# A transformer layer on one core: one product of the last matrix multiply, its order, and three sets of loads are rearranged

## The chip, the cores and the metric

The kernel runs on one core of one Trainium2 chip. The core has five engines with an instruction queue each: TensorE (PE) multiplies matrices, VectorE (DVE), ScalarE (ACT) and GpSimd (POOL) work on tiles, and SyncE (SP) issues the transfers between device memory and on-chip memory. Every queue is worked off in order, and an instruction that waits holds up all that stand behind it in its queue. Matrix products are summed in PSUM banks, here of 512 f32 columns.

The metric is device time in microseconds (us) of one execution. Beside the timed runs there is one execution under the hardware profiler, whose trace is read here.

## The reference

One layer of a model with 2048 tokens of width 1024, all in f32: a modulated norm, a projection to retention and attention heads, both mixers, an output projection, and then a feed-forward block that most of this document is about:

```python
x = x + g1 * (jnp.concatenate([ret, att], axis=-1) @ w_out)
h2 = _modulate(_rmsnorm(x, norm2_g), sh2, sc2)
x = x + g2 * (jnp.square(jax.nn.relu(h2 @ w_ff1)) @ w_ff2)   # 1024 -> 4096 -> 1024
return _rmsnorm(x, final_norm_g)
```

## The kernel before

**Arithmetic.** An f32 operand is split into an f16 part and an f16 remainder ("hi" and "lo"): ACT writes hi, and DVE or POOL writes lo. One product then takes three f16 matmuls: hi by hi, hi by lo, lo by hi. Both products of the feed-forward block are besides done with seven block products instead of eight (names P1 to P7): blocks are added and subtracted on POOL before, partial sums after. `ONTO` says which products are accumulated onto the PSUM bank of another: P6, P7 and P4 onto P1's, P3 onto P5's. In between, the running sum is read out ("tapped") for those output blocks that need it.

**Order.** The program is written out by hand. In the feed-forward block one step is one product: 12 matmuls of 512 columns, 4 blocks of the inner dimension by 3. A function call is put at a step and into a phase, and the phases of a step are emitted in the order

```python
FPHASES = ("begin", "pe", "sum", "hi", "lo", "relu", "out", "square", "late", "dma")
```

so `on(k + 1, "hi", f)` stands on its engine after all that belongs to step k. Nothing reorders it later. Tiles come from pools with a fixed number of buffers; a `Ring` strings several pools together and hands their buffers out in turn. A new tile waits until the last reader of its buffer is done.

**Up stage.** `w_ff1` is used in 16 blocks of 256 columns. `fetch_w1` loads a block in two tiles (names `w1r`), POOL adds (`sum_w1`, tiles `w1s`), ACT and DVE split (`w1f`). The token halves' seven forms (`hf`, 1 MB each) are loaded once. `up_out` taps a product on ACT (tile `r`), adds on DVE, squares on ACT, and `store_u` writes the result. `prelude` is the start of the stage: it loads the forms and does the first four products while the end of the attention part is still running. `w2_forms` runs beside blocks 8 to 15 and after: for each of the 16 row blocks of `w_ff2` it fetches two tiles (`b`), multiplies them by the gate on POOL, forms sums (`bs`), splits them (`w2f`) and stores them for the down stage (`wf`). The first tiles of the down stage's weights (`w`, `fetch_w2`) are loaded in the later part of the up stage.

**Down stage.** Four rounds of the inner dimension (`rd`), each with four passes `c`; a pass works on two pairs of token tiles (e = 0, 1), so there are 16 passes. `down` does P1, P6, P5, P7 and P3 for both pairs, 12 matmuls each. For P2 and P4 (`DEEP`) the two pairs are taken together and split once more, rows by pair, inner dimension and columns by halves: seven small products (`small`) of 6 matmuls with 256 columns, in four steps; POOL forms their sums in `sum_deep`. `down_out` and `small_out` add the PSUM sums to the output tiles `y`: directly on DVE (`plus`), or by ACT into a tile `d` that POOL adds (`tap`). In the last round `made` and `ending` finish each token tile: a sum of squares per half (ACT, `square`), the root on POOL, the final scaling of 1024 columns on DVE (`whole`), and the store (`out`). `P1`'s sums use a ring of 2 banks ("pc"), all others one of 6 ("pd").

Steps are counted from `NU`, the first of the down stage; pass c begins at step NU + 10 c. `STEPS` is the order of a pass's products; P2's small ones run with its first four steps and P4's from the sixth.

## Time and profile before

| | us |
|---|---|
| median of 3 runs | 2633.44 (2630.14 to 2634.4) |
| profiled execution, its own time | 2631.15 |
| span of its trace, first to last instruction | 2629.4 |
| TensorE busy in the span | 2574.5 (98%) |
| VectorE / GpSimd / ScalarE busy | 2170.5 / 1902.0 / 1608.5 |
| granted TensorE clock, mean | 0.997 |

By the trace the first matmul of the up stage starts at 1448.6, the first of the down stage at 2044.5, and the last round begins at 2466.6; the last matmul begins at 2617.5. In the lists of waits a line reads: engine, tile and line that waited, the engine, tile and line that released it, the total in us, the number of times, and the longest. In the timeline a row is start, duration, engine, line, instruction; a bracket gives the engine's idle time just before it and the releaser. In the table of windows a row gives the stretch and its length, then each engine's busy time and number of instructions, the granted clock, the busy share of the DMA engines and GB/s.

### The profile page before, as it was taken

Reading aid. Unit: us, or ns where it says so; the run is one execution under the profiler, and the core shown is the slowest. Engines: PE = TensorE matmul, PEld = TensorE weight load, DVE = VectorE, ACT = ScalarE, POOL = GpSimd, SP = SyncE. Lnnn points to the kernel's source line nnn. Section 1 sums busy time; section 2 is a strip of 40 time slices with the busy share of each in tenths; the row PEclk is TensorE's granted clock in tenths of the full one; section 3 lists DMA queues with packets and bytes.
Section 4 is the critical chain, followed back from the end, with each engine's and each line's share of the span. In section 5 each row is a group of like instructions: output and inputs, shape, how many; then the busy total and the mean of one; then the engine's idle time right before and its main releaser. Section 6 shows DMA issues by size and latency. Waiting matters only on the chain.

```text
span 2629.4 us, 47072 instructions
## 1 busy us (share of the span) xinstructions
PE 2574.5 (98%) x17193; PEld 1506.0 (57%) x17193; DVE 2170.5 (83%) x3160; ACT 1608.5 (61%) x2819; POOL 1902.0 (72%) x1611
## 2 busy tenths in 40 slices
PE   8999999998999999999999999999999999999997
PEld 5885555546666666666666444444444555555544
DVE  5778799769888888888885686899974789988898
ACT  3865454327778878887887676766766443333443
POOL 3644577627666678788787686899874688888886
PEclk9999999999999999999999999999999999999999
DMA  7877899756121223333333656777785768584741
GB/s 232 283 241 236 272 345 350 231 145 211 46 89 57 70 84 84 94 97 113 93 85 129 236 153 188 241 241 241 220 303 172 268 218 305 171 309 174 259 169 65
DMA packets 344816, 494.54 MB, mean 188 GB/s; under 512 B 90868, under 2 KB 215044, under 8 KB 340104
## 3 DMA queue, kind: packets, MB, share of 16 engines
q1 hardware_dynamic: 344568, 491.53, 56.7%
q8 instruction: 135, 2.21, 0.3%
q14 instruction: 97, 0.79, 0.1%
q10 hardware_dynamic: 16, 0.01, 0.0%
HBM read 328.18 MB, written 162.67 MB: 187 GB/s over the span
## 4 chain that ended last, share of the span: by engine, by line
PE 77%; DVE 8%; DMA 4%; POOL 4%; ACT 3%; issue 3%; SPq 0%; DVEq 0%; ACTq 0%; POOLq 0%
PE pso L1202 5%; PE pso L1203 5%; PE pso L1204 5%; PE pd L2407 5%; PE pd L2405 5%; PE pd L2406 5%; PE pu L2089 4%; PE pu L2091 4%; PE pu L2090 4%; PE st L219 4%; PE st L220 4%; PE o L254 4%; PE mp L186 4%; PE o L252 2%; DVE w2f L2209 2%
## 5 line engine op out<-in xcount | busy, mean ns | idle before, releaser
L199 DVE TENSOR_REDUCE nm<-mp 128x1 f32<-128x512 f32 x558 | 377.6, 684 | 97.6 <-PE mp L186 89.5
L225 ACT ACTIVATE p<-st 128x512 f32<-128x512 f32 x576 | 338.8, 594 | 140.1 <-PE st L220 139.3
L236 POOL TENSOR_TENSOR plo<-p,phi 128x1024 f16<-128x1024 f32 x160 | 348.2, 2182 | 70.5 <-ACT phi L229 69.3
L2089 PE MATMUL pu<-hf,w1f 128*128 128x512 f16 x896 | 340.2, 380 | 11.0 <-ACT r L2100 10.9
L2091 PE MATMUL pu<-hf,w1f 128*128 128x512 f16 x896 | 340.3, 380 | 0.0
L2090 PE MATMUL pu<-hf,w1f 128*128 128x512 f16 x896 | 340.2, 380 | 0.0
L229 ACT ACTIVATE phi<-p 128x1024 f16<-128x1024 f32 x288 | 302.8, 1051 | 0.0
L2405 PE MATMUL pd<-w,uf 128*128 128x512 f16 x640 | 242.6, 379 | 0.0
L2406 PE MATMUL pd<-w,uf 128*128 128x512 f16 x640 | 242.6, 379 | 0.0
L2407 PE MATMUL pd<-w,uf 128*128 128x512 f16 x640 | 242.6, 379 | 0.0
L238 DVE TENSOR_TENSOR plo<-p,phi 128x512 f16<-128x512 f32 x256 | 227.3, 889 | 15.2 <-ACT phi L229 13.4
L252 PE MATMUL o<-wv,plo 128*128 128x65 f16 x2304 | 230.0, 193 | 0.9 <-POOL plo L236 0.9
L254 PE MATMUL o<-wv,phi 128*128 128x129 f16 x2176 | 228.3, 220 | 0.0
L2439 ACT ACTIVATE d<-pd,scy 128x512 f32<-128x512 f32 x96 | 65.9, 687 | 261.6 <-PE pd L2407 256.2
L219 PE MATMUL st<-qr,ks 128*128 128x512 f16 x576 | 218.1, 379 | 3.7 <-ACT p L225 3.6
L252 PEld LDWEIGHTS <-plo 128*128 128x128 f16 x2304 | 205.1, 98 | 27.9 <-POOL plo L236 2.0
L2440 POOL TENSOR_TENSOR y<-y,d 128x512 f32<-128x512 f32 x96 | 148.5, 1547 | 98.1 <-ACT uf L2389 91.0
L220 PE MATMUL st<-qr,ks 128*128 128x512 f16 x576 | 218.2, 379 | 0.1
L1202 PE MATMUL pso<-wf,h_l 128*128 128x512 f16 (+1 forms) x576 | 208.2, 361 | 0.0
L1203 PE MATMUL pso<-wf,h_l 128*128 128x512 f16 (+1 forms) x576 | 208.1, 361 | 0.0
L1204 PE MATMUL pso<-wf,h_l 128*128 128x512 f16 (+1 forms) x576 | 208.1, 361 | 0.0
L254 PEld LDWEIGHTS <-phi 128*128 128x128 f16 x2176 | 193.1, 97 | 24.2
(414 smaller groups left out, 7025.7 us busy)
## 6 DMA issues: line engine op xcount, KB each, us to landing
wm<-in_w_ff SPq DMA_DIRECT2D x64, 512.0 KB, 6.7
u<-r SPq DMA_DIRECT2D x128, 256.0 KB, 4.5
wf<-w2f SPq DMA_DIRECT2D x128, 256.0 KB, 4.2
ur<-u SPq DMA_DIRECT2D x128, 256.0 KB, 5.8
y<-x SPq DMA_DIRECT2D x64, 512.0 KB, 6.9
w<-wf SPq DMA_DIRECT2D x28, 1024.0 KB, 6.7
w1r<-in_w_ff SPq DMA_DIRECT2D x48, 512.0 KB, 4.5
x<-y SPq DMA_DIRECT2D x48, 512.0 KB, 2.8
```

Source lines behind the costliest of these rows:

```text
L199: nc.vector.tensor_reduce(dst, src, axis=AX.X, op=ALU.max, negate=True)
L236: nc.gpsimd.tensor_tensor(lo, p, hi, op=ALU.subtract)
L252: mm(o[:, : HD + 1], lo[:, i, c], v[:, : HD + 1], start=False, stop=False)
L254: mm(o, hi[:, i, c], v[:, :VW], start=False, stop=last)
L1202: mm(ps[:, :width], hi[:, k], wh, start=k == 0, stop=False)
L1203: mm(ps[:, :width], hi[:, k], wl, start=False, stop=False)
L2089: mm(ps, whi, hi, start=k == 0 and at == i, stop=False, **go_on)
L2090: mm(ps, whi, lo, start=False, stop=False, **go_on)
L2091: mm(ps, wlo, hi, start=False, stop=k == 3, **go_on)
L2405: mm(ps, u[:, 0, b], w[:, b, 0], start=b == 0 and at == i, stop=False, **go_on)
L2406: mm(ps, u[:, 0, b], w[:, b, 1], start=False, stop=False, **go_on)
L2407: mm(ps, u[:, 1, b], w[:, b, 0], start=False, stop=b == 3, **go_on)
```

## The change

Five things are changed.

1. In the last round only P2 keeps the second level (`DEEP` becomes a list by round). P4 there is done for each pair directly, 12 matmuls of 512 columns, onto P1's bank. Its weights are written to memory without the second level's sums.
2. The order of the last round's products: P1 and P6 of both pairs, then P5, P7, P3, P4 of the first pair, then the same four of the second. A pass there has 12 steps instead of 10 (`START`). The final scaling of a second pair is written 3 steps later than it would follow, except in the very last.
3. In rounds 0 to 2, P7's sum is added to its two output blocks from PSUM by DVE (`plus` twice), not through ACT's tile `d` with an add each on POOL and DVE.
4. `w_ff1`'s second block is fetched 9 steps earlier and into buffers of the tag "hb".
5. `w2_forms` fetches its blocks 3 steps earlier, has four `bs` buffers instead of three, and does most of the second-level splits a step or two later; the down stage's first seven weight tiles are loaded every 6 steps instead of every 3.

Three small ones: `junk` comes from the ring of `d`, `bn` has two buffers, and the ring of the down stage's raw blocks has the new `bs` buffer too.

```diff
+    BLOCK = {P2: "a12", P4: "a22"}
+    DEEP = [(P2, P4)] * 3 + [(P2,)]
...
+        ff["bs"] = Ring((xp, "hu", 3), (ff["k"], "bs", 1))
...
-            w = xp.tile([P, D], F32, name="w1r", tag="xr", bufs=XR).rearrange("p (k n) -> p k n", k=4)
+            tag, bufs = ("hb", HB) if n == 1 else ("xr", XR)
+            w = xp.tile([P, D], F32, name="w1r", tag=tag, bufs=bufs).rearrange("p (k n) -> p k n", k=4)
...
-            on(b0 - 5 + g, "dma", fetch, g)
+            on(b0 - (8 if gate else 5) + g, "dma", fetch, g)
...
-                on(k + 1, "hi", hold)
-                split(k + 1, to[:, 0:4:3, s], lambda f: pieces(f, x[w][:, L], kept[i][:, L]))
+                on(k + 2, "hi", hold)
+                split(k + 2, to[:, 0:4:3, s], lambda f: pieces(f, x[w][:, L], kept[i][:, L]))
...
-            split(k + 1, to[:, 2:5:2, s], lambda f: pieces(f, kept[i]))
-            split(k + 2, to[:, 1:6:4, s], lambda f: pieces(f, x[w]))
-            on(k + 3, "sum", minus, held(L), part(L), held(L))
-            split(k + 4, to[:, 6, s], lambda f: pieces(f, kept[i][:, L]))
+            split(k + 2, to[:, 2:5:2, s], lambda f: pieces(f, kept[i]))
+            split(k + 3, to[:, 1:6:4, s], lambda f: pieces(f, x[w]))
+            on(k + 4, "sum", minus, held(L), part(L), held(L))
+            split(k + 6, to[:, 6, s], lambda f: pieces(f, kept[i][:, L]))
...
-        on(k0 + 10, "dma", fetch_w1, 1)
+        on(k0 + 1, "dma", fetch_w1, 1)
...
-            on(first[NB, 0] + 2 + 3 * i, "dma", fetch_w2, i)
+            on(first[NB, 0] + 2 + 6 * i, "dma", fetch_w2, i)
...
-    STEPS = [(i, e) for i in (P1, P6, P5, P7, P3) for e in range(2)]
+    STEPS = [[(i, e) for i in (P1, P6, P5, P7, P3) for e in range(2)]] * 3
+    STEPS += [STEPS[0][:4] + [(i, e) for e in range(2) for i in (P5, P7, P3, P4)]]
+    S3, S4 = [(0, 1)] * 3 + [(0, 4)], [(3, 4)] * 3 + [(1, 5)]
+    START = [10 * c if c < 13 else 12 * c - 24 for c in range(16)]
...
         elif i == P7:
-            d = tap(1, 1)
-            on(at + 1, "out", lambda: nc.vector.tensor_tensor(y[1, 0], y[1, 0], d, op=ALU.add))
+            if P4 in DEEP[PAIRS[p][0]]:
+                plus(1, 1)
+                plus(1, 0)
+            else:
+                tap(1, 1)
             made(at + 1, p, 1, 1)
+        elif i == P4:
+            plus(1, 0)
+            made(at, p, 1, 0)
...
-            junk = ff["sm"].tile([P, 512], BF16, name="junk", tag="junk", bufs=1)
+            junk = ff["d"].tile([P, 512], F32, "junk")
...
-            on(at + 1, "lo", whole, c)
-            on(at + 1 if n == 2 else at + 3, "dma" if n == 1 else "lo", store, c)
+            late = 3 if p % 2 and p < len(PAIRS) - 1 else 0
+            on(at + 1 + late, "lo", whole, c)
+            on(at + 1 if n == 2 else at + 3 + late, "dma" if n == 1 else "lo", store, c)
```

Three places show what this moves. A row is a line of the code, an instruction and its tiles; xN stands for N like it in a row.

SP's queue at the start of the up stage, before (`hf` are the seven forms, `w1r` the block of `w_ff1`, `x` a store of the attention part's result):

```order
L2076 DMA hf<-hf_230 128x4096
L2076 DMA hf<-hf_231 128x4096
L2076 DMA hf<-hf_232 128x4096
L2076 DMA hf<-hf_233 128x4096
L2076 DMA hf<-hf_234 128x4096
L1861 DMA x_212<-xr 128x1024
L2045 DMA w1r<-in_w_ff 128x4x256 x2
```

And now:

```order
L2079 DMA hf<-hf_230 128x4096
L2079 DMA hf<-hf_231 128x4096
L2048 DMA w1r<-in_w_ff 128x4x256 x2
L2079 DMA hf<-hf_232 128x4096
L2079 DMA hf<-hf_233 128x4096
L2079 DMA hf<-hf_234 128x4096
L1862 DMA x_212<-xr 128x1024
```

The two transfers of the second block stand ahead of the last three forms and of the store.

SP's queue in the later part of the up stage, before (`w` are the down stage's weights, `b` the tiles of `w2_forms`, `u` stores of the up stage's results):

```order
L2343 DMA w_24960<-wf_243 128x4096
L2132 DMA u_237<-r 128x4x128
L2213 DMA wf_270<-w2f 128x2x512
L2132 DMA u_238<-r 128x4x128
L2213 DMA wf_270<-w2f 128x512
L2343 DMA w_25021<-wf_244 128x4096
L2132 DMA u_240<-r 128x4x128
L2141 DMA b<-in_w_ff 128x1024
L2045 DMA w1r<-in_w_ff 128x4x256 x2
L2141 DMA b<-in_w_ff 128x1024
L2343 DMA w_25094<-wf_245 128x4096
```

And now:

```order
L2350 DMA w_24947<-wf_243 128x4096
L2135 DMA u_237<-r 128x4x128
L2144 DMA b<-in_w_ff 128x1024
L2135 DMA u_238<-r 128x4x128
L2144 DMA b<-in_w_ff 128x1024
L2135 DMA u_240<-r 128x4x128
L2048 DMA w1r<-in_w_ff 128x4x256 x2
L2350 DMA w_25076<-wf_244 128x4096
```

Both `b` tiles stand ahead of the second weight tile and of `w1r`, and the last stores of the second level (`wf_270`) are gone.

DVE's queue in the last round, where one pass ends and the next begins, before (L2500 is the final scaling, L2464 the read of a small product, L2435 the read of a large one, L2393 the lo part of a split, L2451 the add of `d`):

```order
L2435 SCALAR_TENSOR_TENSOR y<-pd,scy,y 128x512
L2393 TENSOR_TENSOR uf<-us,uf 128x512 x2
L2500 SCALAR_TENSOR_TENSOR y<-y,cy_e,g2b 128x1024 x2
L2464 SCALAR_TENSOR_TENSOR y<-pd,scy,y 128x256 x2
L2393 TENSOR_TENSOR uf<-us,uf 128x512
L2393 TENSOR_TENSOR uf<-ur,uf 128x256
L2500 SCALAR_TENSOR_TENSOR y<-y,cy_e,g2b 128x1024 x2
L2464 SCALAR_TENSOR_TENSOR y<-pd,scy,y 128x256 x2
```

And now (the same operations are L2512, L2476, L2442 and L2400):

```order
L2442 SCALAR_TENSOR_TENSOR y<-pd,scy,y 128x512
L2400 TENSOR_TENSOR uf<-us,uf 128x512 x2
L2476 SCALAR_TENSOR_TENSOR y<-pd,scy,y 128x256 x2
L2400 TENSOR_TENSOR uf<-us,uf 128x512
L2400 TENSOR_TENSOR uf<-ur,uf 128x256
L2476 SCALAR_TENSOR_TENSOR y<-pd,scy,y 128x256 x2
L2400 TENSOR_TENSOR uf<-us,uf 128x512
L2476 SCALAR_TENSOR_TENSOR y<-pd,scy,y 128x256 x2
L2400 TENSOR_TENSOR uf<-ur,uf 128x512
L2512 SCALAR_TENSOR_TENSOR y<-y,cy_e,g2b 128x1024
L2476 SCALAR_TENSOR_TENSOR y<-pd,scy,y 128x256
```

Two of the four final scalings that stood ahead of a pass's first two reads of small products now stand one by one behind the third pair of reads; the other two stand in the middle of the pass.

More of the change, by code (lines that the diff above doesn't have):

```diff
@@ L107, in layer_kernel @@
     ONTO = {P6: P1, P7: P1, P4: P1, P3: P5}
-    DEEP = {P2: "a12", P4: "a22"}
+    BLOCK = {P2: "a12", P4: "a22"}
+    DEEP = [(P2, P4)] * 3 + [(P2,)]
     wf_d = [
         [
-            dram.tile([P, 7, 2, 512] if i in DEEP else [P, 4, 2, 512], F16, name=f"wf{rd}{i}", tag=f"wf{rd}{i}")
+            dram.tile([P, 7, 2, 512] if i in DEEP[rd] else [P, 4, 2, 512], F16, name=f"wf{rd}{i}", tag=f"wf{rd}{i}")
             for i in range(7)
@@ L1684, in stats @@
             if 0 in hs:
-                x["st", c] = sm.tile([P, 4, 6], F32, name="bn", tag="bn")
+                x["st", c] = sm.tile([P, 4, 6], F32, name="bn", tag="bn", bufs=2)
                 x["mv", c] = sm.tile([P, 4, 2], F32, name="mv", tag="mv")
@@ L2149, in add @@
         def add(to, p, q, at=None):
-            x[to] = x[at] if at else xp.tile([P, 512], F32, name="bs", tag="hu", bufs=3)
+            x[to] = x[at] if at else ff["bs"].tile([P, 512], F32, "bs")
             nc.gpsimd.tensor_tensor(x[to], x[p], x[q], op=ALU.subtract)
         for g in range(2):
-            on(b0 - 5 + g, "dma", fetch, g)
+            on(b0 - (8 if gate else 5) + g, "dma", fetch, g)
             if gate:
@@ L2339, in fetch_w2 @@
             ff["w2"] = Ring((ff["h"][1], "hf", 7), (ff["h"][0], "hf", 7))
-        rd, (i, part) = n // 9, WS[n % 9]
+        rd, i, part, _ = WS[n]
         w = w2[rd, i, part] = ff["w2"].tile([P, 4, 2, 512], F16, "w2")
@@ L2345, in open_down @@
     def open_down():
[L2346 removed]
+        ff["raw"] = Ring((xp, "w1s", W1S), (xp, "hu", 3), (ff["k"], "bs", 1))
         ff["us"] = Ring((xp, "hp", HP), (xp, "u", 2), (ff["k"], f"k{P2}", 1), (ff["k"], f"k{P4}", 1))
@@ L2370, in sum_deep @@
     def sum_deep(c, i, which):
-        a1, a2 = (raw2[2 * c + e, DEEP[i]] for e in range(2))
+        a1, a2 = (raw2[2 * c + e, BLOCK[i]] for e in range(2))
         L, R = slice(0, 2), slice(2, 4)
@@ L2431, in down_out @@
         ps = pu[e, ONTO.get(i, i)]
-        y = {(g, n): ys[p, g][:, n * 512 : (n + 1) * 512] for g in range(2) for n in range(2)}
+        y = {(g, n): ys[p, g][:, n * 512 : (n + 1) * 512] for g in range(2) if (p, g) in ys for n in range(2)}
         def plus(g, n):
@@ L2507, in ending @@
             c = slice(i * D // n, (i + 1) * D // n)
-            on(at + 1, "lo", whole, c)
-            on(at + 1 if n == 2 else at + 3, "dma" if n == 1 else "lo", store, c)
+            late = 3 if p % 2 and p < len(PAIRS) - 1 else 0
+            on(at + 1 + late, "lo", whole, c)
+            on(at + 1 if n == 2 else at + 3 + late, "dma" if n == 1 else "lo", store, c)
     def down_jobs():
-        for n in range(36):
+        for n in range(7, len(WS)):
             if n < 9:
-                at = NU + n - 12
+                at = n - 12
             elif n < 14:
-                at = NU + 2 * n - 14
+                at = 2 * n - 14
             else:
-                at = NU + 10 * (4 * ((n - 14) // 9) + 3) + USED[(n - 14) % 9] + 1
-            if n > 6:
-                on(at, "dma", fetch_w2, n)
+                rd, _, _, used = WS[n - 14]
+                at = START[4 * rd + 3] + used + 1
+            on(NU + at, "dma", fetch_w2, n)
         on(NU - 12, "begin", open_down)
@@ L2525, in down_jobs @@
         for c in range(len(PAIRS) // 2):
-            s, p = NU + 10 * c, (2 * c, 2 * c + 1)
+            s, p = NU + START[c], (2 * c, 2 * c + 1)
+            rd = PAIRS[2 * c][0]
             for at, blk, e in ((-10, 0, 0), (-10, 0, 1), (-9, 1, 1), (-9, 1, 0), (-8, 2, 0), (-8, 3, 0), (-7, 2, 1), (-7, 3, 1)):
@@ L2533, in down_jobs @@
                 on(s - 2 + e, "sum", sum_u, p[e], "s2", "s1", "a11", ALU.subtract)
-                on(s + e, "sum", sum_u, p[e], "s3", "a11", "a21", ALU.subtract, "a21")
-                on(s + 3 + e, "sum", sum_u, p[e], "s4", "a12", "s2", ALU.subtract, "s2")
-            for k, i in ((-5, P2), (0, P4)):
+                on(s + S3[rd][e], "sum", sum_u, p[e], "s3", "a11", "a21", ALU.subtract, "a21")
+                on(s + S4[rd][e], "sum", sum_u, p[e], "s4", "a12", "s2", ALU.subtract, "s2")
+            for k, i in zip((-5, 0), DEEP[rd]):
                 for m in range(4):
                     on(s + k + m, "sum", sum_deep, c, i, m + 1)
-            for j, (i, e) in enumerate(STEPS):
+            for j, (i, e) in enumerate(STEPS[rd]):
                 split_u(s + j - 3, (c, i, e), lambda p=p[e], i=i: raw2[p, FORMS1[i]])
@@ L2542, in down_jobs @@
                 on(s + j, "out", down_out, s + j, c, i, e)
-            for k, i in ((0, P2), (5, P4)):
-                a1, a2 = (lambda p=q, i=i: raw2[p, DEEP[i]] for q in p)
+            for k, i in zip((0, 5), DEEP[rd]):
+                a1, a2 = (lambda p=q, i=i: raw2[p, BLOCK[i]] for q in p)
                 split_u(s + k - 3, (c, i, "ab"), a1)
```

9 lines of the change are left out of this document (4 added, 5 removed).

## The prediction

> **What bounds the kernel now.** I read the page first:
>
> ```profile
> span 2629.4 us, 47072 instructions
> PE 2574.5 (98%) x17193; PEld 1506.0 (57%) x17193; DVE 2170.5 (83%) x3160; ACT 1608.5 (61%) x2819; POOL 1902.0 (72%) x1611
> ```
>
> TensorE is busy 98% of the span. So only two things can matter: how much TensorE has to do, and the 55 us in which it does nothing. The list of TensorE's waits says where the larger part of those is:
>
> ```profile
> PE pd L2423 <- DVE y L2464: 10.9, 7, 1.8
> PE pu L2089 <- ACT r L2100: 10.9, 5, 3.9
> ```
>
> Five stalls in the up stage and seven in the down stage, 21.8 us. The rest is the start, which this change does not touch, and the end behind the last matmul. I looked at each of the three places in the timeline.
>
> **1. The second block of w_ff1.** The longest stall is at the start of the up stage (first fence), and it has a second cost:
>
> ```profile
> 1464.07 0.38 PE L2089 MATMUL pu<-hf,w1f 128*128 128x512 f16 x1 [3.94 <-ACT r L2100]
> 1464.55 0.63 PE L2091 MATMUL pu<-hf,w1f 128*128 128x512 f16 x1
> 1467.91 0.38 PE L2090 MATMUL pu<-hf,w1f 128*128 128x512 f16 x1
> 1464.00:1468.00 4.00, 3.93 (x11) 1.49 (x11) 1.43 (x2) 2.06 (x5) 4.00 (x4) 0.57 0.44 128
> ```
>
> After 3.94 us of idleness the granted clock is 0.57 in the next 4 us (last row, third number from the end). From 1464.55 to 1467.91 only eight matmuls start. At the usual pace of 0.216 us (below) they take 1.73, so 1.6 us more are lost. The cause is a load:
>
> ```profile
> 1435.51 9.13 SPq L2076 DMA_DIRECT2D hf<-hf  x7
> 1452.10 1.03 SPq L2045 DMA_DIRECT2D w1r<-in_w_ff  x2
> 1461.54 0.72 ACT L2062 ACTIVATE w1f<-w1r,sc 128x512 f16<-128x512 f32 x1 [6.76 <-DMA w1r<-in_w_ff]
> ```
>
> SP issues the block at 1452.10, behind seven forms and a store; ACT waits for it till 1461.54, and the tap that TensorE needs stands behind that wait on ACT. Now the block stands behind the fourth form, so it is issued some 11 us earlier, and ACT meets data that is there: **-3.94 and -1.6**. What it costs: the last three forms land later by 1 MB of w1r, one seventh of what the seven took, under 3 us. Their first user is the product that stalls now, so a form that came late would give back part of the 3.94; I take none. Bounds: 0 if the "hb" buffer is not free, -5.6 else. Both buffers were last read for forms that must be stored before the loads of the seven, so I take the full **-5.6**.
>
> **2. The later part of the up stage.** From 1880 to 1970 TensorE, ACT and POOL wait as follows, and the last row is the window in which the transfers are densest early on:
>
> ```profile
> PE pu L2089 <- ACT r L2100: 6.9, 4, 3.3
> ACT w2f L2205 <- POOL w2k L2228: 13.5, 6, 6.4
> POOL b L2147 <- DMA b<-in_w_ff: 18.7, 4, 10.5
> 1900.00:1920.00 20.00, 20.00 (x94) 9.06 (x93) 10.21 (x15) 12.88 (x22) 6.00 (x6) 1.00 1.01 336
> ```
>
> Read from the bottom: the DMA engines are full (1.01), because the early weight tiles of the down stage, 1 MB each, stand among the fetches of `b`. POOL waits 18.7 us for `b`, then ACT 13.5 us for POOL's second-level sums, and the tap behind it makes TensorE wait 6.9. The change acts on each link: `b` is fetched 3 steps (7.8 us) earlier and ahead of the second weight tile, the weight tiles come half as often, the ACT split is written a step later, and all four blocks of this stretch belong to round 3, whose P4 sums, splits and stores vanish. I take **-6.3**, nine tenths of the 6.9; bounds 0 and -6.9. Where the stall goes: what is late next is the weight tiles themselves, the last now issued 18 steps (47 us) ahead of the down stage, which covers a load of 7 us.
>
> An earlier fetch can also wait for its buffer. The tiles fetched at 1735.47 take the buffers that DVE last reads in the row of 1724.25:
>
> ```profile
> 1724.25 3.98 DVE L2209 TENSOR_TENSOR w2f<-b,w2f 128x512 f16<-128x512 f32 x2
> 1735.47 0.38 SPq L2141 DMA_DIRECT2D b<-in_w_ff  x1
> ```
>
> They are free at 1728.23, and 7.8 us before 1735.47 is 1727.7. SP waits some 0.5 us, with the stores of `u` queued behind it: no cost to TensorE, but no slack either (a rival below).
>
> **3. The last round.** Six of the seven waits of the down stage are here:
>
> ```profile
> PE pd L2423 <- DVE y L2464: 9.8, 6, 1.8
> 2506.99 2.48 DVE L2500 SCALAR_TENSOR_TENSOR y<-y,cy_e,g2b 128x1024 f32<-128x1024 f32 x2
> 2509.39 1.06 DVE L2464 SCALAR_TENSOR_TENSOR y<-pd,scy,y 128x256 f32<-128x256 f32 x2
> 2509.91 0.27 PE L2423 MATMUL pd<-w,uf 128*128 128x256 f16 x1 [1.59 <-DVE y L2464]
> ```
>
> Two final scalings stand on DVE ahead of the read of a small product, whose bank the next small product reuses. In the new order the first three pairs of reads have no scaling ahead of them: **-9.8**.
>
> TensorE's own work grows. The pace comes from three starts, 12 small matmuls and then 12 large ones:
>
> ```profile
> 2469.19 0.27 PE L2423 MATMUL pd<-w,uf 128*128 128x256 f16 x1
> 2470.50 0.38 PE L2405 MATMUL pd<-w,uf 128*128 128x512 f16 x1
> 2473.09 0.27 PE L2423 MATMUL pd<-w,uf 128*128 128x256 f16 x1
> ```
>
> 1.31/12 = 0.109 us and 2.59/12 = 0.216 us. P4 took 42 small matmuls, 4.58 us; now it takes 24 large ones, 5.18. In four passes **+2.4**. A pass is 12 x 2.59 + 4.58 = 35.7 us.
>
> Do the other engines keep up with 35.7? One period of the last round before (38.57 us, from stall to stall), ten passes of the earlier rounds, and DVE's groups in that period:
>
> ```profile
> 2511.22:2549.79 38.57, 35.39 (x206) 19.94 (x204) 37.29 (x44) 18.71 (x40) 35.03 (x31) 1.00 0.47 164
> 2100.00:2450.00 350.00, 350.00 (x2039) 199.29 (x2037) 316.43 (x380) 134.66 (x241) 291.54 (x221) 1.00 0.68 241
> L2393 DVE TENSOR_TENSOR uf<-us,uf 128x512 f16<-128x512 f32 x11 | 14.1, 1291 | 0.0
> L2464 DVE SCALAR_TENSOR_TENSOR y<-pd,scy,y 128x256 f32<-128x256 f32 x14 | 6.4, 474 | 1.1 <-PE pd L2425 0.9
> L2435 DVE SCALAR_TENSOR_TENSOR y<-pd,scy,y 128x512 f32<-128x512 f32 x4 | 3.0, 741 | 0.0
> L2451 DVE TENSOR_TENSOR y<-y,d 128x512 f32<-128x512 f32 x2 | 1.7, 834 | 0.2
> ```
>
> DVE, 37.3: off go P4's seven reads (3.3), two adds of `d` (1.7) and four splits, one of them half (some 4.5); on come two splits (2.6) and two reads (1.5): 31.9 of 35.7. POOL, 35.0: off go four 256-wide sums, 0.73 to 1.18 each (row below): 31 of 35.7. Both fit. Two banks now turn over faster: P3 follows its pair's P5 with one product between, 2.59 us, into which one read of 0.74 must fall behind a split and a scaling. I add **+0.8** for stalls there; bounds 0 and 9.8.
>
> In rounds 0 to 2 DVE gets four reads (3.0) for two adds (1.7), so 31.6 a pass becomes 32.9 of 35; POOL loses two adds a pass. TensorE does not wait in those ten passes at all (350.00 busy of 350.00), and I take 0; bounds 0 and +6.
>
> A rule speaks against the last round. POOL's and DVE's tile operations disturb each other; alone and together they take (shortest, median and longest in ns):
>
> ```profile
> L2393 DVE TENSOR_TENSOR uf<-us,uf x156: 673/1212/1765, 2052.9 to 2608.5; 128x512 f16<-128x512 f32 x156
> L2440 POOL TENSOR_TENSOR y<-y,d x96: 1258/1711/1743, 2052.4 to 2611.4; 128x512 f32<-128x512 f32 x96
> L2384 POOL TENSOR_TENSOR us<-ur x61: 716/726/1182, 2053.7 to 2594.2; 128x256 f32<-128x256 f32 x61
> L2500 DVE SCALAR_TENSOR_TENSOR y<-y,cy_e,g2b x18: 746/1274/1742, 2507.0 to 2622.9; 128x1024 f32<-128x1024 f32 x14, 128x512 f32<-128x512 f32 x4
> ```
>
> If such operations exclude each other for their whole length, a pass of the new last round needs, at their shortest, POOL's 14 full and 4 half ones (20.5) with some 3 for the four roots (one operation of a root takes 1.56 under a scaling, part 4), and DVE's 15.5 splits (10.4) and 4 scalings (5.1): 39 us, 3.3 above 35.7. In passes 13 and 14, which carry this whole load, that is +6.6 and a time of some 2617. The same count for the period before gives 14 full, 8 half, the roots, 17 splits, 2 adds and 4 scalings, 44 against 38.57 measured, so they overlap in part, and I do not take it. The Trainium skill states this exclusion (SBUF — State Buffer, section "SBUF: two separate sides": the pair of ports that VectorE and GpSimd share is a lock held for a whole instruction); by that sum these rows disagree.
>
> **4. The end.** Times from the last matmul's end at 2617.77:
>
> ```profile
> 2617.54 0.23 PE pd L2407
> 2618.53 5.12 DVE L2500 SCALAR_TENSOR_TENSOR y<-y,cy_e,g2b 128x1024 f32<-128x1024 f32 x6
> 2619.53 1.56 POOL L2494 TENSOR_SCALAR cv_e<-ss 128x1 f32<-128x1 f32 x1 [1.18 <-ACT junk L2483]
> 2621.69 3.32 SPq L2503 DMA_DIRECT2D out<-y  x6
> out<-y SPq DMA_DIRECT2D x4, 256.0 KB, 2.0
> ```
>
> Behind it come 11.6 us: six scalings, a root that POOL does in their shadow, six stores of 2 MB. Now the first pair is done four steps earlier. Left are the read (0.75), sum of squares (0.8), the root (some 1.1, under the first half tile's scaling), two half scalings of 0.75, and a store of 256 KB, 2.0 to landing. With 0.1 between links the last half is scaled at +4.5 instead of +5.9 (2618.53 + 5.12), issued 0.35 later and landed at +6.9. In the old end 2.4 us lie between the last issue with that landing time (2621.69 + 3.32 + 2.0) and the end of the span; part of it is the queue of 2 MB, and I take 1.5: 8.4. **-3.2**; bounds -2 and -4.4.
>
> **Sum**, against the profiled execution's own 2631.15 (its span is 2629.4): -5.6 - 6.3 - 9.8 + 2.4 + 0.8 - 3.2 = -21.7, so 2609.4. That execution lies inside the three runs (2630.14 to 2634.4, median 2633.44), so a median of new runs lies about there or a little above: **2610**.
>
> **Rivals.**
> - *The last round stays bound by DVE and POOL*: the sum of 39 holds in passes 13 and 14 and TensorE waits 3.3 in each, or the reads of P5 and P7 come late by about as much. For it: both engines over 90% busy before. Against: 3.8 us of room on DVE. Price +7 to +9: 2618. Chance 0.14.
> - *The up stage keeps its stalls*, because DVE, full from 1880 to 1900, is late whatever POOL does: 2610 + 6.3 = 2616. Chance 0.1.
> - *Rounds 0 to 2 start to stall*, DVE having one microsecond more a pass: half a microsecond in 12 passes, 2616. Chance 0.1.
> - *Slower than before*: the earlier fetch of `b` waits for its buffer in each of 14 blocks, the stores of `u` wait behind it on SP, the nine `r` tiles run out, and ACT's taps stop TensorE. It decides once SP waits longer than about 8 us, three steps, in which four of the nine `r` tiles are due; 2 us in each block is 28: 2638. The row of 1724.25 allows 0.5 us of waiting, so 0.03.
>
> Forecast 0.58; the rest, 0.05, are mixtures. From the forecast's bounds (2604 with all stalls gone and -4.4 at the end, 2613) to the rivals at 2616 and 2618 the range is 2603 to 2620. A measurement tells 0.2% (5.3 us) from no change. Only the last rival and a mixture reach it: faster 0.93, same 0.04, slower 0.03.
>
> **What would show it.** The wait of 3.94 and the clock of 0.57 are gone at the start of the up stage, and w1r is issued near 1440. POOL's waits for `b` are short past 1900, and TensorE is busy throughout. In the last round no L2464-like wait remains and passes are 35.7 apart; DVE is at 90% or less. The span ends 8 to 9 us behind the last matmul. I am wrong if a new wait of the large products on DVE appears in the last round, if rounds 0 to 2 take more than 35.0 a pass, or if SP waits in front of `b`.

## The result

| | before | after |
|---|---|---|
| median of the runs (us) | 2632.73 (2630.14 to 2634.4) | 2619.19 (2617.96 to 2620.43) |
| ratio, 95% interval | | 0.9949 (0.9932 to 0.9967) |
| profiled execution, its own time | 2631.15 | 2618.28 |
| span of its trace | 2629.4 | 2616.4 |

The change makes the kernel 13.5 us faster. That lies inside the range of the prediction, at its upper end, 9 us above the forecast of 2610. So more than a third of the expected gain is missing, and the first question is where.

The page of the changed kernel, and its list of TensorE's waits (engine, tile and line that waited, who released it; total us, times, longest):

```profile
span 2616.4 us, 46757 instructions
PE 2577.8 (99%) x17121; PEld 1499.6 (57%) x17121; DVE 2133.8 (82%) x3142; ACT 1594.3 (61%) x2779; POOL 1842.2 (70%) x1563
```

```profile
PE pu L2092 <- DVE r L2107: 9.4, 2, 7.1
...
PE pu L2092 <- ACT r L2103: 1.6, 2, 1.1
...
PE pd L2412 <- DVE y L2442: 0.6, 3, 0.2
```

The waits of the down stage have gone from 10.9 us to 0.6. Those of the up stage were 10.9 and are 11.0: one of them now lasts 7.1 us. The two profiled executions, stretch by stretch, by the start of the first matmul of each:

| stretch | before | after | difference | predicted |
|---|---|---|---|---|
| until the up stage (code hardly touched) | 1448.6 | 1446.5 | -2.1 | 0 |
| up stage, first 126 matmuls | 35.0 | 38.5 | +3.5 | -5.6 |
| rest of the up stage | 560.8 | 559.1 | -1.7 | -6.3 |
| rounds 0 to 2 | 422.1 | 420.8 | -1.3 | 0 |
| last round to its last matmul | 150.8 | 143.6 | -7.2 | -6.6 |
| behind the last matmul | 11.6 | 7.5 | -4.1 | -3.2 |
| sum | | | -12.9 | -21.7 |

The down stage and the end did what was forecast, the up stage did not. The first row is code in which only `bn`'s second buffer and the early transfer are new; the up stage starts at 1446.5 to 1451.7 in the twelve experiments below, so the difference is scatter between executions, and stretches are compared from their own start.

The two rows of the up stage scatter as well. Of the experiments below, e4 and e12 have this stage as in the kernel before, e3, e5 and e6 as in the changed one. The first 126 matmuls take 35.0, 36.0 and 36.1 in the three traces of the old stage and 38.5, 39.0, 37.9 and 38.0 in the four of the new; the rest takes 560.8, 564.8 and 562.1 against 559.1, 559.1, 559.0 and 557.4. By these means the differences are +2.6 and -3.9 rather than +3.5 and -1.7.

**The start of the up stage, after.** The timeline of the changed kernel: SP's queue, the links of the chain, and TensorE:

```profile
1438.18 1.19 SPq L2048 DMA_DIRECT2D w1r<-in_w_ff  x2
1439.42 6.67 SPq L2079 DMA_DIRECT2D hf<-hf  x3
1449.57 0.32 SPq L1862 DMA_DIRECT2D x<-xr  x1
1460.68 1.12 POOL L1872 TENSOR_SCALAR xr<-xr,cy_f 128x1024 f32<-128x1024 f32 x1 [9.22 <-DMA x<-xr]
1462.76 1.26 POOL L2060 TENSOR_TENSOR w1s<-w1r 128x512 f32<-128x512 f32 x1
1466.27 1.95 ACT L2065 ACTIVATE w1f<-w1s,sc 128x512 f16<-128x512 f32 x3 [7.61 <-POOL w1s L2060]
1469.60 0.68 DVE L2107 TENSOR_TENSOR r<-pu,r 128x512 f32<-128x512 f32 x1
1470.33 0.58 PE L2092 MATMUL pu<-hf,w1f 128*128 128x512 f16 x1 [7.12 <-DVE r L2107]
```

and a row of its table of windows:

```profile
1468.00:1472.00 4.00, 1.67 (x5) 0.55 (x5) 4.00 (x6) 2.62 (x5) 1.13 (x1) 0.50 1.02 328
```

The second block of `w_ff1` is issued at 1438.18 as planned, and ACT no longer waits for it. But POOL scales `xr` in place, and may do so only when the store of `x` out of that tile has landed. That store is issued at 1449.57 and lands 11 us later, behind the forms and the block. Then POOL makes the sums `w1s` of the second block, ACT and DVE split them, DVE adds a product that stands behind the split in its queue, and only then TensorE has a bank again. It idles 7.12 us, and its clock is granted at 0.50 afterwards (third number from the end of the last row).

Was that chain there before? Yes, and it was on time by a hair:

```profile
1460.27 1.12 POOL L1871 TENSOR_SCALAR xr<-xr,cy_f 128x1024 f32<-128x1024 f32 x1 [6.70 <-DMA x<-xr]
1470.39 0.68 DVE L2104 TENSOR_TENSOR r<-pu,r 128x512 f32<-128x512 f32 x1
1470.71 0.38 PE L2091 MATMUL pu<-hf,w1f 128*128 128x512 f16 x1
1471.13 0.38 PE L2089 MATMUL pu<-hf,w1f 128*128 128x512 f16 x1
```

These are the same instructions in the kernel before. DVE is through at 1471.07, TensorE starts at 1471.13, 0.42 behind the matmul before it instead of 0.216: it had already waited 0.2 us for this chain. That matmul, the 73rd of the stage, starts 22.49 us behind the first one before and 23.79 after. The wait of 3.94 us that was removed had only covered this one. Of the 3.5 us that the 126 matmuls lose, 1.3 are lost up to this matmul; the other 2.2 are lost behind it, where the clock is granted at 0.50: the remaining matmuls take 14.7 us instead of 12.5.

### The profile page after: what moved, and what is told of

The parts are those of the page before. It is cut to its first block, busy times and chain, and to the rows that moved or that the text cites. A ratio compares the mean times of both kernels' runs of the same rounds, so it can differ in the third digit from the quotient of the medians.

```text
span 2616.4 us, 46757 instructions
## 1 busy us (share of the span) xinstructions
PE 2577.8 (99%) x17121; PEld 1499.6 (57%) x17121; DVE 2133.8 (82%) x3142; ACT 1594.3 (61%) x2779; POOL 1842.2 (70%) x1563
## 5 line engine op out<-in xcount | busy, mean ns | idle before, releaser
L2412 PE MATMUL pd<-w,uf 128*128 128x512 f16 x672 | 254.7, 379 | 0.6 <-DVE y L2442 0.6
L2414 PE MATMUL pd<-w,uf 128*128 128x512 f16 x672 | 254.7, 379 | 0.0
L2413 PE MATMUL pd<-w,uf 128*128 128x512 f16 x672 | 254.7, 379 | 0.0
L2447 POOL TENSOR_TENSOR y<-y,d 128x512 f32<-128x512 f32 x72 | 107.3, 1493 | 136.0 <-ACT uf L2396 126.1
L187 PE MATMUL mp<-ks,qr 128*128 128x512 f16 x512 | 194.0, 379 | 1.4 <-DVE nm L200 0.6
```

What stands on the lines that cost most here:

```text
L2412: mm(ps, u[:, 0, b], w[:, b, 0], start=b == 0 and at == i, stop=False, **go_on)
L2413: mm(ps, u[:, 0, b], w[:, b, 1], start=False, stop=False, **go_on)
L2414: mm(ps, u[:, 1, b], w[:, b, 0], start=False, stop=b == 3, **go_on)
```

## The experiments

Each is the kernel named with the edit shown; e9 and e10 join two, and e11 undoes several. The ratio is to runs of the kernel before on the same chip, whose median there lay between 2632.4 and 2635.2; "up" is the time from the first matmul of the up stage to the first of the down stage, "down" from there to the start of the last matmul, "end" what follows that matmul's end.

| run | median (us) | ratio (95%) | up | down | end |
|---|---|---|---|---|---|
| before | 2632.73 | | 595.8 | 572.9 | 11.6 |
| after | 2619.19 | 0.9949 (0.9932 to 0.9967) | 597.6 | 564.4 | 7.5 |
| e1, three forms later | 2612.27 | 0.9922 (0.9906 to 0.9939) | 589.3 | 564.4 | 7.5 |
| e2, w_ff1's block late again | 2615.98 | 0.9935 (0.9921 to 0.9950) | 592.2 | 564.4 | 7.5 |
| e3, scaling not delayed | 2620.03 (one run) | | 598.0 | 565.4 | 7.5 |
| e4, before + delayed scaling | 2646.04 | 1.0049 (1.0034 to 1.0064) | 600.7 | 585.6 | 11.6 |
| e5, pairs interleaved | 2619.82 | 0.9946 (0.9931 to 0.9961) | 596.9 | 564.8 | 8.8 |
| e6, P7 through ACT's tile | 2619.39 | 0.9944 (0.9929 to 0.9958) | 595.4 | 566.0 | 7.5 |
| e7, b late again | 2617.18 | 0.9935 (0.9921 to 0.9950) | 592.6 | 564.4 | 7.5 |
| e8, weight tiles dense again | 2619.08 | 0.9944 (0.9927 to 0.9961) | 596.0 | 564.4 | 7.5 |
| e9, both of these | 2616.75 | 0.9940 (0.9925 to 0.9955) | 593.1 | 564.4 | 7.5 |
| e10, e1 and e7 together | 2609.23 | 0.9913 (0.9898 to 0.9928) | 585.3 | 564.4 | 7.5 |
| e11, last round as before | 2622.32 | 0.9964 (0.9949 to 0.9978) | 594.6 | 566.4 | 11.6 |
| e12, before + P7 from PSUM | 2626.09 | 0.9966 (0.9953 to 0.9978) | 598.2 | 566.3 | 11.6 |

### The start of the up stage: e1 and e2

e1 fetches the last three forms behind the store of `x`, with the block of `w_ff1` still early:

```diff
-            on(k0 + i // 2, "dma", fetch_h, i)
+            on(k0 + i // 2 if i < 4 else made_at + 1, "dma", fetch_h, i)
```

> The changed kernel, with the last three forms (P7, P3, P4 of hf) loaded behind the store of x instead of ahead of it. Theory (the new stall of 7.1 us at the start of the up stage hangs on that store: it stands behind 8 MB in the queue, POOL waits 9.2 us for it before it may form w1's sums, and the sums are what ACT, DVE and then TensorE wait for): the store lands some 3 us after its issue, POOL starts 6 to 8 us earlier, the stall and the slow clock behind it go, -8 to -9 us, some 2610.5. Rival 1 (the store takes 11 us whatever is ahead of it, or POOL's sums wait for something else): the stall stays, 0. Rival 2 (the forms now come too late for the fifth product): a stall on the forms' transfer of 1 to 4 us takes its place, -4 to -8.

Measured: 2612.27, 7 us less than the changed kernel. The same chain in its timeline:

```profile
1450.90 0.34 SPq L1862 DMA_DIRECT2D x<-xr  x1
1451.28 1.78 SPq L2079 DMA_DIRECT2D hf<-hf  x3
1454.68 1.32 POOL L1872 TENSOR_SCALAR xr<-xr,cy_f 128x1024 f32<-128x1024 f32 x1 [1.89 <-ACT w1f L2065]
1465.46 0.38 PE L2092 MATMUL pu<-hf,w1f 128*128 128x512 f16 x1 [0.93 <-DVE r L2107]
```

The store, issued ahead of the three forms, lands within 4 us; POOL's `xr` starts 3.8 us behind the issue instead of 11.1, and TensorE waits 0.93 instead of 7.12, with no loss of clock. So the queue in front of the store of `x` made the new wait, and no wait for the later forms takes its place. The first 126 matmuls take 30.1 us, 4.9 less than before.

e2 undoes the fetch of the second block alone:

```diff
-            tag, bufs = ("hb", HB) if n == 1 else ("xr", XR)
-            w = xp.tile([P, D], F32, name="w1r", tag=tag, bufs=bufs).rearrange("p (k n) -> p k n", k=4)
+            w = xp.tile([P, D], F32, name="w1r", tag="xr", bufs=XR).rearrange("p (k n) -> p k n", k=4)
...
-        on(k0 + 1, "dma", fetch_w1, 1)
+        on(k0 + 10, "dma", fetch_w1, 1)
```

> The changed kernel with part 4 undone (w_ff1's second block fetched where it was, into the old buffers). Theory (the early fetch removed one wait and uncovered a longer one on POOL's sums, by delaying the store of x): the wait of 3.9 us with its slow clock comes back in place of the 7.1 with its slow clock, -3 us, some 2616. Rival, as predicted before the result (the early fetch is worth 5.6 us, and the long wait has another cause, the other edits or this run): +5.6 us on top of the 7.1, or no change at all.

Measured: 2615.98. The old wait is back, and yet the kernel is 3.2 us faster than with the early fetch:

```profile
1466.62 0.38 PE L2092 MATMUL pu<-hf,w1f 128*128 128x512 f16 x1 [3.71 <-ACT r L2103]
```

Part 4 of the change, as it stands, is a loss. Together with the forms moved as in e1, the early fetch is 3.7 us better than e2, which has neither. The forms moved alone, with the block still late, were not run, so how the 3.7 us divide between the two is not shown.

### The last round: e3, e4, e5, e11 and e12

The last round gave what was predicted. The question was which part of the change gave it. I had said: the scalings no longer stand ahead of the reads of the small products. e3 takes the delay of the scalings away from the changed kernel. e4 gives the kernel before a delay alone, there for both pairs of token tiles and not only for the second:

```diff
-            late = 3 if p % 2 and p < len(PAIRS) - 1 else 0
+            late = 0
```

> The changed kernel with the final scaling of a second pair written where it would follow (the shift by 3 steps undone), the new order and the direct P4 kept. Theory (place: what stands on DVE ahead of the first reads of small products decides): one scaling of 1.2 to 1.4 us instead of two stands ahead of each of two reads; two cost 1.6 to 1.8 us, so the slack was 0.7 and one costs 0.4 to 0.6, twice in three passes: waits of small products of some 3 us in total. Rival (load: the stalls came from DVE having more than it could do in a pass, and P4's removal cured them): no such waits, 0.

```diff
-        v, r = (sm.tile([P, 1], F32, name=f"c{x}_e", tag=f"c{x}_e") for x in "vy")
+        v, r = (sm.tile([P, 1], F32, name=f"c{x}_e", tag=f"c{x}_e", bufs=6) for x in "vy")
...
-            on(at + 1, "lo", whole, c)
-            on(at + 1 if n == 2 else at + 3, "dma" if n == 1 else "lo", store, c)
+            late = 3 if p < len(PAIRS) - 2 else 0
+            on(at + 1 + late, "lo", whole, c)
+            on(at + 1 if n == 2 else at + 3 + late, "dma" if n == 1 else "lo", store, c)
```

> The kernel before, with one edit: in the last round all final scalings but those of the last pass are written 3 steps later (and the tiny root tiles have more buffers, which that needs). P4's second level and the order stay. Theory (place): the six waits of 9.8 us go without the 2.4 us of added TensorE work, -8 to -10 us against before. Rival (load): DVE is busy 37.3 us of a period of 38.6 and cannot do that in the 35.1 that a pass takes TensorE, so at least 2 us in each of three passes come back elsewhere: -3 us at most.

Measured, e3: three waits of 0.54 us return and the down stage takes 1.0 us more, which lies between the theory's 3 us and the rival's 0. e4: the kernel becomes 13 us slower than before, where both theories had it faster. DVE and TensorE in one place of e4's last round (for e4 the line numbers are those of before):

```profile
2521.26 3.96 DVE L2500 SCALAR_TENSOR_TENSOR y<-y,cy_e,g2b 128x1024 f32<-128x1024 f32 x2
2525.15 0.47 DVE L2464 SCALAR_TENSOR_TENSOR y<-pd,scy,y 128x256 f32<-128x256 f32 x1
2525.54 1.36 DVE L2393 TENSOR_TENSOR uf<-ur,uf 128x512 f16<-128x512 f32 x1
2526.83 1.76 DVE L2393 TENSOR_TENSOR uf<-us,uf 128x512 f16<-128x512 f32 x1
2528.51 3.95 DVE L2500 SCALAR_TENSOR_TENSOR y<-y,cy_e,g2b 128x1024 f32<-128x1024 f32 x2
2536.37 0.37 PE L2423 MATMUL pd<-w,uf 128*128 128x256 f16 x1 [6.19 <-DVE y L2464]
```

and the next period in its table of windows:

```profile
2536.37:2580.40 44.03, 37.55 (x205) 20.81 (x205) 37.73 (x42) 18.56 (x40) 36.46 (x31) 0.93 0.41 143
```

A pair of scalings takes 3.95 us where it took 2.48 before: the delayed ones stand beside an unbroken row of POOL's operations. In the 44.03 us of the period DVE is busy 37.73 and idle the rest, waiting for TensorE in turn (38.57 and 37.29 before). The clock adds to it: it is granted at 0.93 in this row (third number from the end), and of the 12.7 us that the down stage takes more than before, longer waits are 6.7. A delay that makes room at one read takes it from the next reads. So a delay of the scalings is not what cured the last round, as far as these two runs show; other places for them were not tried.

e5 keeps P4 direct, but takes the pairs in the old, interleaved order:

```diff
-    STEPS += [STEPS[0][:4] + [(i, e) for e in range(2) for i in (P5, P7, P3, P4)]]
+    STEPS += [STEPS[0] + [(P4, e) for e in range(2)]]
```

> The changed kernel, with P4 at one level in the last round, but with the two pairs' products interleaved as before (P5, P5, P7, P7, P3, P3, P4, P4 of the two pairs). It tells whether the end (7.5 us behind the last matmul instead of 11.6) comes from ending the pairs one by one, as I argued, or from P4's form. My theory: with P4 of the two pairs as the last two products, the first pair's second tile is finished 2.6 us before the second pair's, so DVE has one scaling of 1.3 to 2.5 us more in the end: the end grows by 2 to 4 us, 2621 to 2623 (2619.2 with the order). The rival: the two reads of P4's bank are the end in any order, and the end stays within 1 us: 2619 to 2620. Either order has the same matmuls, so the passes stay at 36.0.

Measured: 0.4 us more in the down stage, 1.3 more behind the last matmul, the median unchanged (2619.82). The order carries the smaller part of the gain at the end; the rival is nearer.

e11 puts the whole last round back as it was and keeps all else. Its core:

```diff
-    DEEP = [(P2, P4)] * 3 + [(P2,)]
+    DEEP = [(P2, P4)] * 4
...
-    STEPS += [STEPS[0][:4] + [(i, e) for e in range(2) for i in (P5, P7, P3, P4)]]
-    S3, S4 = [(0, 1)] * 3 + [(0, 4)], [(3, 4)] * 3 + [(1, 5)]
-    START = [10 * c if c < 13 else 12 * c - 24 for c in range(16)]
+    S3, S4 = [(0, 1)] * 4, [(3, 4)] * 4
+    START = [10 * c for c in range(16)]
...
-            late = 3 if p % 2 and p < len(PAIRS) - 1 else 0
+            late = 0
```

> The changed kernel with the last round as before (P4 at a second level, the pairs interleaved, no delay of the scalings, places 10 apart) and all else as changed: P4's second-level sums, splits and stores for round 3 are back in the up stage too. My theory: the down stage's six waits return (9.8 us), TensorE's work falls by 2.4, and the end grows by 4; if the smaller work for round 3 is what cured the late up stage, waits of 3 to 5 us return between 1930 and 1970: 2632 to 2635 in all. The rival: the up stage stays as it is (one of the loads cures it), 2619.2 + 11.4 = 2629 to 2631.

Measured: 2622.32, much less lost than either theory had it. Only three of the six waits are there, although the scalings stand ahead of the reads as before:

```profile
2511.26 0.27 PE L2428 MATMUL pd<-w,uf 128*128 128x256 f16 x1 [1.20 <-DVE y L2474]
2548.40 0.27 PE L2428 MATMUL pd<-w,uf 128*128 128x256 f16 x1 [1.60 <-DVE y L2474]
2585.54 0.27 PE L2428 MATMUL pd<-w,uf 128*128 128x256 f16 x1 [1.59 <-DVE y L2474]
```

What is left in this kernel is P7, which DVE now adds from PSUM in the last round too, since P4 has its second level there again. e12 does that alone in the kernel before:

```diff
-            d = tap(1, 1)
-            on(at + 1, "out", lambda: nc.vector.tensor_tensor(y[1, 0], y[1, 0], d, op=ALU.add))
+            plus(1, 1)
+            plus(1, 0)
```

> The kernel before, with one part of the change alone: P7 is added by DVE from PSUM (two adds) in all four rounds, in place of ACT's copy, POOL's add and DVE's add of that copy. With the last round undone, the changed kernel still lost only 4.4 us to waits there instead of 9.8, and this part is what was left in. My theory now: the adds from PSUM take 0.74 us whatever POOL does, the add they replace takes up to 1.7 beside POOL, and POOL has an operation less, so in the last round three waits of 1.2 to 1.6 us remain instead of six: 9.8 - 4.4, and the wait of 1.14 us at 2087 goes: 6 to 7 us in all, 2626 to 2627. The rival: the waits left in that run were few for another reason (the places of the w2 loads, the banks of the change), and this part alone is worth nothing, as it was in rounds 0 to 2: 2631 to 2633.

Measured: 2626.09, a ratio of 0.9966 (0.9953 to 0.9978). From its list of waits:

```profile
PE pd L2423 <- DVE y L2464: 4.3, 3, 1.6
```

Three waits remain, 4.3 us instead of 9.8, the wait of 1.14 us in round 0 is gone, and the down stage takes 566.3 us instead of 572.9. An edit of two lines gives 6.6 of the 8.5 us that the down stage won. (Against the runs of the kernel before on the same chip, 2635.22 in the median, it is 9.1 us; the trace accounts for 6.6 of them.)

### Rounds 0 to 2: e6

```diff
             if P4 in DEEP[PAIRS[p][0]]:
-                plus(1, 1)
-                plus(1, 0)
+                d = tap(1, 1)
+                on(at + 1, "out", lambda: nc.vector.tensor_tensor(y[1, 0], y[1, 0], d, op=ALU.add))
```

> The changed kernel, with P7 of rounds 0 to 2 added as before (a copy by ACT, one add on POOL, one add on DVE, instead of two adds from PSUM on DVE). My prediction took nothing for this part, with DVE 1.3 us fuller in each pass; measured, DVE became 1.6 us a pass emptier and POOL 3.3. Theory now: adds from two SBUF tiles are stretched beside POOL's operations and adds from PSUM are not, so with the old form both engines go back to 31.6 and 29.2 us a pass, and TensorE, which had room before, waits only where it did (1.14 us near the down stage's start): 2619 to 2621. The rival: this part is worth more than nothing, since the last round's forms are prepared earlier: 2624 or more.

Measured: 2619.39, the changed kernel's time. Ten passes of the earlier rounds, in e6 first and then after (busy us of PE, PEld, DVE, ACT, POOL):

```profile
2100.00:2450.00 350.00, 350.00 (x2039) 199.29 (x2037) 315.62 (x381) 134.58 (x241) 291.60 (x220) 1.00 0.67 239
```

```profile
2100.00:2450.00 350.00, 350.00 (x2036) 199.00 (x2034) 300.69 (x401) 127.98 (x221) 258.29 (x201) 1.00 0.67 241
```

With the adds from PSUM, DVE does 20 operations more and is busy 15 us less; POOL is busy 33 us less. TensorE is busy throughout in both, so it is worth nothing there, but for one wait near 2088 (1.41 us in e6).

### The late up stage: e7, e8, e9 and e10

```diff
-            on(b0 - (8 if gate else 5) + g, "dma", fetch, g)
+            on(b0 - 5 + g, "dma", fetch, g)
```

> The changed kernel, with the fetch of b back at 5 places ahead of its block instead of 8, and the w2 tiles still spread. It tells which of the two loads cured the waits past 1880 us of the up stage (6.9 us before, 3.9 now). If the earlier fetch of b did it: POOL waits some 10 us for b once again, and TensorE 3 us more, 2622. If the spread of the w2 tiles did it: within 1 us of 2619.

```diff
-            on(first[NB, 0] + 2 + 6 * i, "dma", fetch_w2, i)
+            on(first[NB, 0] + 2 + 3 * i, "dma", fetch_w2, i)
```

> The changed kernel, with the w2 tiles fetched at every third place again instead of every sixth, and b still fetched 8 places ahead. If the spread of the w2 tiles cured the waits of the late up stage: the transfers are dense at 1900 us again, POOL waits for b or w1r, and TensorE waits 3 us more, 2622. If the earlier fetch of b did it alone: within 1 us of 2619.

e9 has both edits.

> The changed kernel with both loads as before: b fetched 5 places ahead, the w2 tiles at every third place. With one of the two back (the two runs before this), the waits of 1.82 and 3.28 us near 1942 and 1964 us of before did not return. Theory: they were cured by neither load but by the smaller work for round 3 (no second-level sums and splits of P4 in these blocks), so they stay away, and the wait of 2.29 us near 1949, which the early fetch of b makes, is gone: 2616 to 2618. The rival: either load alone is enough, and with both back the dense transfers of before return: the waits come back, 4 to 5 us, 2621 to 2624.

Measured: e7 is not slower but 2 us faster than the changed kernel (2615.82 to 2618.24 against 2617.96 to 2620.43, so the runs just overlap), e8 the same, e9 2.4 us faster. The waits of 1.82 and 3.28 us near 1942 and 1964 of before return in none of them; in e9 one of 0.61 at 1975 is left beside that of 1.12 at 1902. In the changed kernel there is one of 2.29, and it is gone in e7, so the early fetch of `b` is needed for it. How it comes about is read from the two traces. In the changed kernel POOL finds both `b` tiles there and gates them without a break; DVE's splits beside it are long, and the add that TensorE needs stands behind them:

```profile
1944.12 1.75 DVE L2071 SCALAR_TENSOR_TENSOR w1f<-w1s,sc,w1f 128x512 f16<-128x512 f32 x1
1945.28 2.79 POOL L2150 TENSOR_TENSOR b<-b,g2b 128x1024 f32<-128x1024 f32 x1
1945.79 2.83 DVE L2212 TENSOR_TENSOR w2f<-bs,w2f 128x512 f16<-128x512 f32 x1
1948.54 0.68 DVE L2107 TENSOR_TENSOR r<-pu,r 128x512 f32<-128x512 f32 x1
1949.27 0.59 PE L2092 MATMUL pu<-hf,w1f 128*128 128x512 f16 x1 [2.29 <-DVE r L2107]
```

In e7 POOL waits for `b` once again (its timeline):

```profile
1947.70 2.36 POOL L2150 TENSOR_TENSOR b<-b,g2b 128x1024 f32<-128x1024 f32 x1 [5.29 <-DMA b<-in_w_ff]
```

and in that pause DVE does five operations in 2.84 us (its table of windows):

```profile
1944.00:1948.00 4.00, 4.00 (x20) 1.85 (x19) 2.84 (x5) 2.44 (x5) 0.30 (x1) 1.00 1.08 389
```

POOL's wait was not a loss but DVE's opportunity. The early fetch does not make the wait by itself, though: e11 has it too, with P4's forms of round 3, and no wait near 1949. What did cure the old waits stays open: with both loads back and P4's round-3 forms gone (e9) they are away, and with the loads changed and those forms back (e11) they are away too (1.40 at 1891 and 1.12 at 1903 is all). Either is enough, or it is what all these kernels share with the changed one, the later splits and the fourth `bs` buffer; those were not undone in any run.

e10 joins the edits of e1 and e7.

> The changed kernel with the two places mended that lost time: the last three forms fetched behind the store of x (worth 7 us alone, 2612.3), and the fetch of b back at 5 places ahead (worth 2 us alone). If the two gains lie in different stretches and add, 2610 (2609 to 2611), with no wait above 1.2 us left past 1440. If they do not add, for instance since the shifted start of the stage moves the loads against the work, 2612.

Measured: 2609.23, ratio 0.9913 (0.9898 to 0.9928), the fastest of all and 10 us below the changed kernel. The gains add, 3.0 us below e1: in the up stage 589.3 becomes 585.3. One wait of 1.75 at its start, which the expectation did not have, and one of 1.11 are left in it.

## Why the prediction was right or wrong

**Step 1, the second block of w_ff1: wrong.** Predicted -5.6, measured +3.5 over the first 126 matmuls. The failing sentence is the one on the bounds: "0 if the 'hb' buffer is not free, -5.6 else". The buffer was free, and the whole was still not to be had, since I took the wait that ended last and did not ask what was next. The trace of before had the answer in POOL's wait of 6.70 us for the store of `x` and in the 0.06 us between the end of DVE's add and the matmul. The block, put ahead of that store, then made the next link later as well: I counted the forms that land later, but not the store behind them, though it stood in the very rows I showed. e1 and e2 show it: with the store behind the block and all the forms the fetch is a loss of 3.2 us; with the last three forms behind the store the start of the stage wins 4.9 us. What the moved forms do alone was not run.

**Step 2, the late up stage: the mechanism wrong, the size too large.** The waits fell from 6.9 us to 3.9 instead of to 0.6, and 1.7 us were won of 6.3, or 3.9 by the means above. What failed is the root of the chain: POOL's wait for `b` was to make TensorE wait. In e9, with both loads as before, POOL again waits 14.4 us for `b` between 1880 and 1970, and TensorE's waits past 1880 in that stage come to 1.7. What the cure was stays open (see e9 and e11). The early fetch of `b` costs 2 us, by a mechanism I had not listed: POOL without pauses lengthens DVE's splits. The rival "the up stage keeps its stalls" (2616) comes nearest in mechanism, but it had DVE late whatever POOL does; here DVE was late because of what POOL does. The rival nearest in number, the last round still bound by DVE and POOL (2618), did not come. The rival that SP would wait for `b`'s buffers did not come.

**Step 3, the last round: the size right, the reason wrong.** -9.8 + 2.4 + 0.8 were predicted; -7.2 was measured, with 0.6 us of new waits and a period that contains 36.0 us, against 35.7 worked out. After's row for such a stretch answers the one of 38.57 us shown before:

```profile
2510.00:2546.00 36.00, 35.79 (x187) 18.16 (x186) 33.94 (x33) 17.88 (x38) 32.41 (x27) 1.00 0.51 176
```

DVE is at 33.9 of 36 where 31.9 was worked out: the four scalings in it take 8.1 us, since their new place is beside POOL's operations; the sign "DVE is at 90% or less" did not come. But the gain does not come from the scalings' delay (e3: 1.0 us; e4: a loss), nor from the order (e5: 0.4 us). What is left is the direct form of P4, with the load that it takes off DVE and POOL; no run has it alone, so this is concluded and not shown. As e11 and e12 show, most of the same relief is to be had by the P7 adds alone.

**Rounds 0 to 2: right**, 0 predicted, -1.3 measured, of which 1.14 is the wait in round 0. The working was wrong in sign: DVE did not get 1.3 us a pass more but 1.6 less. I had priced the add of `d` at 0.83 us and taken the splits' durations as fixed; with POOL's adds gone, the splits themselves became shorter. Two groups of DVE from 2060 to 2480, most of rounds 0 to 2, before and after (mean ns of one behind the comma):

```profile
L2393 DVE TENSOR_TENSOR uf<-ur,uf 128x512 f16<-128x512 f32 x71 | 104.6, 1486 | 0.1
L2451 DVE TENSOR_TENSOR y<-y,d 128x512 f32<-128x512 f32 x24 | 23.1, 964 | 2.5
```

```profile
L2400 DVE TENSOR_TENSOR uf<-ur,uf 128x512 f16<-128x512 f32 x72 | 81.0, 1137 | 0.1
L2442 DVE SCALAR_TENSOR_TENSOR y<-pd,scy,y 128x512 f32<-128x512 f32 x96 | 69.0, 738 | 0.4 <-PE pd L2414 0.4
```

**Step 4, the end: the size right, the reason in part**, -3.2 predicted, -4.1 measured; 7.5 us behind the last matmul against 8.4. The rows after:

```profile
2608.96 0.75 DVE L2442 SCALAR_TENSOR_TENSOR y<-pd,scy,y 128x512 f32<-128x512 f32 x1 [1.84 <-PE pd L2414]
2609.62 1.40 DVE L2512 SCALAR_TENSOR_TENSOR y<-y,cy_e,g2b 128x512 f32<-128x512 f32 x2
2611.87 1.42 DVE L2512 SCALAR_TENSOR_TENSOR y<-y,cy_e,g2b 128x512 f32<-128x512 f32 x2 [0.84 <-POOL cy_e L2507]
```

The last scaling ends 4.4 us behind the last matmul's end at 2608.92, as worked out (4.5). I had put it down to the order of the pairs. Of the 4.1 us the order gives 1.3 (e5); e11, with P4 in its old form and order, has the old 11.6, so the remaining 2.8 goes with P4's form.

So the forecast was too fast by the two terms of the up stage, 9.1 and 4.6 us, less some 5 that came back from scatter, the earlier rounds, the last round and the end (2.1 + 1.3 + 0.6 + 0.9). That the time still lies in the range is in part luck: the range's upper end came from rivals that did not happen, the up stage's loss had no place in it, and 2.1 us of the gain in this pair of traces are scatter.

## What to carry to other kernels

A wait that ends last is worth no more than the distance to the wait that ends next. Before its full length is booked, the other engines' idle times in the same microseconds must be read, hidden ones too. When a transfer is moved up, every transfer that it passes must be followed to its reader, stores whose tile is overwritten included. Where VectorE and GpSimd are both nearly full, as here, an add that reads PSUM is worth trying in place of one with two operands in SBUF, and a pause of GpSimd is not to be closed without asking which VectorE operation uses it. An experiment that does one part alone belongs beside one that undoes it: the same relief can come from two parts, and undoing either shows too little. And before a stretch of one trace is explained, other traces of the same code tell its scatter: here the same up stage took 595.8, 598.2 and 600.7 us.
